# Feed-forward without row products, the overflow branch two experts earlier, and the second block's vectors loaded in the attention

## The chip, the cores and the metric

The kernel runs on one core of a Trainium2 chip. The metric is the device time of one execution in microseconds. A core has a matmul engine (TensorE, PE in the profile, its weight loads PEld), VectorE (DVE), ScalarE (ACT), GpSimd (POOL) and SyncE (SP), which issues the DMA transfers. Each engine runs its own queue in order; semaphores tie the queues together.

## The reference

The model takes x of 256 tokens by 1024, in float32. A first block has two layers: a state-space mixer (layer 0) and a differential attention (layer 1), each followed by a mixture of 32 experts of which every token uses two, with layer norms between. A second block has two layers of a three-part attention and a gated feed-forward. What the change touches:

```python
def hier_moe(x, w_group, w_expert, w_gate, w_up, w_down):     # twice; 32 experts, top 2
    ...
    h = jax.nn.silu(xb @ w_gate[e]) * (xb @ w_up[e])          # 1024 -> 512
    return h @ w_down[e]                                      # 512 -> 1024

def rms_norm(x, g):
    y = xf * lax.rsqrt(jnp.mean(xf * xf, axis=-1, keepdims=True) + NORM_EPS_2)
    return (y * g).astype(x.dtype)

# second block, twice
h = rms_norm(x, g_ffn[l])
u = causal_dwconv(h @ w_up[l], conv_w[l], conv_b[l])          # 1024 -> 5632, three taps over the tokens
gate, up = u[..., :D_FF], u[..., D_FF:]                       # D_FF = 2816
x = x + (jax.nn.silu(gate) * up) @ w_down[l]
```

## The kernel before

The stages follow each other: state-space layer (to about 262 us of the profile), first mixture (to 706), attention (to 850), second mixture (to 1295), then twice an attention mixer and a feed-forward layer, and a last norm. All queues' orders are set when the program is built: a scheduler simulates the engines and orders each queue, so an edit can shift neighbours too.

**Weights** come in pages of 1 MB through `ws`: SyncE issues a load as soon as a page is free and runs ahead of the use by as many pages as there are. `ws.take` and `ws.give` lend a page to other uses.

**Precision.** A float32 weight is split into a high part (ScalarE's cast, line 247) and the rest (a subtraction, line 225, in `low`). Three matmuls, high by high, high by low and low by high (lines 426 to 428), make a product. `low` sends every fourth subtraction to GpSimd and the others to VectorE; with `fast` all go to VectorE. Four buffers hold split weights.

**The mixture** (`moe`). For each expert e: `gate_up` (line 1036) multiplies the gathered tokens with two 1 MB pages each of the gate and up weights, `hidden` forms the gated product, `down` (line 1090) multiplies with the down weights of the expert before. An expert takes up to 32 tokens in this loop. If any expert has more, `overflow` does the rest: all engines load the longest count (line 1162) and take or skip a branch (line 1163) whose body holds the whole code for long experts. Before, it stands behind the last expert, in `moe_layer`, and behind the loads of the next stage's weights; the next thing is `normalize` on the sums `out` (statistics line 519, factors lines 337, 338 and 524, normalized copies line 534 on ScalarE and 536 on VectorE, then transposes, line 204).

**The vectors of the second block** (convolution taps, biases, norm gains) come as rows of 128 numbers: `columns` loads them into staging tiles (line 320) and `finish` transposes these on the matmul engine, copies the result (line 329) and halves some of it (line 2072). `prepare_block2` is a generator that the second mixture resumes at experts 4, 20, 24, 28 and at the end: the loads of layer 0 at the first, those of layer 1 at the second.

**The feed-forward** (`ffn`). xT holds x times the gain, split, by features. The norm's factor `row` is one number per token and is multiplied into the product afterwards. Eleven iterations each take two pages of up weights: 8 weight splits, 96 matmuls into two PSUM accumulators (gate and up), then per accumulator `ff_y` = accumulator times row (line 1742, VectorE), and on two halves of it one tap on ScalarE (line 1748) and two on VectorE (line 1750); then tanh, a gate product on VectorE (line 1755), the product of both on GpSimd (line 1756) and its split into gT (`put_pair`, lines 1810 and 225).

## Time and profile before

| | us |
|---|---|
| median of 3 timed runs | 1997.39 (1997.09 to 1997.48) |
| profiled execution | 1993.87, its span 1992.1 |
| PE busy in the span | 1763.0 (88%) |
| DVE, ACT, POOL busy | 912.1, 856.4, 387.9 |
| first mixture, 262 to 706 | DMA share 0.99, PE busy 363.0 of 444 |
| second mixture, 850 to 1295 | DMA share 0.99, PE busy 358.6 of 445 |
| attention, 706 to 850 | DMA share 0.70, PE busy 129.7 of 144 |
| up projections, 1442 to 1579 and 1777 to 1915.4 | PE busy 130.2 of 137 and 131.3 of 138.4 |

The span is cut into stages because each has another limit: the mean busy share of an engine over the whole span says little about any of them. "Share" of DMA is that of the 16 DMA engines; a share about 1 with a matmul engine that idles is a stage that waits for weights. In rows with a bracket, the first number is the engine's idle time before the instruction, and behind the arrow stands what ended it. A letter q behind an engine's name is its sequencer.

### The profile page before, as it was taken

How to read it: one execution, taken by the hardware profiler on the slowest of the kernel's cores; microseconds unless marked ns; L12 is line 12 of the kernel's file. 1: busy time of each engine (PE TensorE's matmuls, PEld its weight loads, DVE VectorE, ACT ScalarE, POOL GpSimd, SP SyncE). 2: the span in 40 equal slices, each digit the busy share in tenths (PEclk: the TensorE clock that was granted, in tenths of full speed). 3: DMA queues.
4: the chain of work that ended last, by engine and by line, in shares of the span. 5: the costliest groups of instructions: out<-in, count | busy, mean ns of one | idle time of the engine just before them, and what ended most of it. 6: DMA issues, size and time to landing. Idle time of an engine off the chain costs nothing. (4 is left out here: it accounts for less than half of the span.)

```text
span 1992.1 us, 36677 instructions
## 1 busy us (share of the span) xinstructions
PE 1763.0 (88%) x14641; PEld 1388.7 (70%) x14642; DVE 912.1 (46%) x2077; ACT 856.4 (43%) x1940; POOL 387.9 (19%) x329
## 2 busy tenths in 40 slices
PE   8999999787877779999787777779999999999998
PEld 7989876444544467776454444367899997789998
DVE  7888621000100068711000000069589947868983
ACT  5656533121222245633212122256656645656653
POOL 1444300000000023100000000033244423334441
PEclk9999999888989889999889898989999999999999
DMA  9634779999999994799999999974245544424540
GB/s 300 205 127 173 300 307 418 419 418 419 419 419 419 417 335 170 287 368 419 419 419 419 419 373 419 414 264 140 86 156 172 219 145 152 148 86 158 177 174 22
DMA packets 163053, 563.77 MB, mean 283 GB/s; under 512 B 17597, under 2 KB 78652, under 8 KB 114236
## 3 DMA queue, kind: packets, MB, share of 16 engines
q1 hardware_dynamic: 162732, 561.29, 72.8%
q8 instruction: 118, 1.93, 0.4%
q14 instruction: 59, 0.48, 0.1%
q10 hardware_dynamic: 144, 0.07, 0.0%
HBM read 560.27 MB, written 1.05 MB: 282 GB/s over the span
## 5 line engine op out<-in xcount | busy, mean ns | idle before, releaser
L247 ACT CAST w<-w 128x512 fp32r<-128x512 f32 (+1 forms) x592 | 351.6, 610 | 234.2 <-PE acc L256 77.0
L1036 PE MATMUL tr<-w,xe 128*32 128x256 f32 x4096 | 333.5, 426 | 120.3 <-DMA w<-in_moe_w_up_dram 85.5
L225 DVE TENSOR_TENSOR w<-w,w 128x512 fp32r<-128x512 f32 (+1 forms) x450 | 334.1, 755 | 136.8 <-ACT w L247 136.4
L1036 PEld LDWEIGHTS tr<-w,xe 128*32 128x32 f32 x4096 | 150.1, 119 | 273.5 <-DMA w<-in_moe_w_up_dram 120.1
L225 POOL TENSOR_TENSOR w<-w,w 128x512 fp32r<-128x512 f32 (+1 forms) x142 | 199.1, 1402 | 433.0 <-ACT w L247 417.6
L428 PE MATMUL acc<-w,w 128*128 128x256 f32 x960 | 258.1, 286 | 14.8 <-DVE w L225 9.7
L426 PE MATMUL acc<-w,w 128*128 128x256 f32 x960 | 266.6, 283 | 1.5 <-ACT w L247 1.5
L427 PE MATMUL acc<-w,w 128*128 128x256 f32 x960 | 266.4, 283 | 0.0
L428 PEld LDWEIGHTS acc<-w,w 128*128 128x128 f32 x960 | 175.6, 190 | 20.7 <-DVE w L225 14.6
L1071 DVE SCALAR_TENSOR_TENSOR hT<-hT,tr 128x128 f32<-128x128 f32 x64 | 18.4, 288 | 364.1 <-ACT hT L1070 364.1
L426 PEld LDWEIGHTS acc<-w,w 128*128 128x128 f32 x960 | 182.3, 190 | 2.4 <-ACT w L247 1.9
L427 PEld LDWEIGHTS acc<-w,w 128*128 128x128 f32 x960 | 182.4, 190 | 0.5
L1090 PE MATMUL tr<-w,hT 128*32 128x256 f32 x2048 | 154.1, 408 | 30.3 <-DMA w<-in_moe_w_down_dram 22.4
L1045 ACT COPY gu<-tr 128x256 f32<-128x256 f32 x64 | 23.8, 372 | 350.5 <-PE tr L1036 350.5
L255 PE MATMUL acc<-w,w 128*128 128x512 f32 (+3 forms) x416 | 161.4, 390 | 11.1 <-DVE w L225 10.9
L1096 ACT ACTIVATE w<-tr,sw 32x256 f32<-32x256 f32 x248 | 115.6, 466 | 115.4 <-PE tr L1090 98.9
L256 PE MATMUL acc<-w,w 128*128 128x512 f32 (+3 forms) x416 | 153.9, 379 | 0.0
L980 POOL CAST oh<-oh 128x192 fp32r<-128x192 f32 x16 | 5.6, 349 | 738.6 <-DVE oh L977 722.3
L254 PE MATMUL acc<-w,w 128*128 128x512 f32 (+3 forms) x416 | 146.5, 388 | 3.0 <-ACT w L1820 2.0
L478 PE MATMUL acc<-w,w 128*128 128x256 f32 x480 | 134.1, 283 | 0.0
L477 PE MATMUL acc<-w,w 128*128 128x256 f32 x480 | 133.7, 284 | 0.0
L479 PE MATMUL acc<-w,w 128*128 128x256 f32 x480 | 131.7, 285 | 1.5 <-POOL w L225 1.2
(401 smaller groups left out, 2888.6 us busy)
## 6 DMA issues: line engine op xcount, KB each, us to landing
w<-in_moe_w_gate_dram SPq DMA_DIRECT2D x128, 1024.0 KB, 17.6
w<-in_moe_w_up_dram SPq DMA_DIRECT2D x126, 1024.0 KB, 19.9
w<-in_moe_w_down_dram SPq DMA_DIRECT2D x126, 1024.0 KB, 19.9
w<-in_w_up_dram SPq DMA_DIRECT2D x88, 512.0 KB, 5.0
w<-in_w_down_dram SPq DMA_DIRECT2D x22, 1024.0 KB, 6.5
w<-in_w_in_dram SPq DMA_DIRECT2D x18, 1024.0 KB, 8.7
w<-in_ssm_w_in_dram SPq DMA_DIRECT2D x16, 1024.0 KB, 7.6
w<-in_attn_w_qkv_dram SPq DMA_DIRECT2D x12, 1024.0 KB, 10.8
```

Of the source, the lines that this page charges most:

```text
L225: eng.tensor_tensor(lo, x, hi.bitcast(F32), op=ALU.subtract)
L247: self.nc.scalar.copy(hi, w)
L254: mm(out, lhs[0], rhs[0], start=start, stop=False)
L255: mm(out, lhs[0], rhs[1], start=False, stop=False)
L256: return mm(out, lhs[1], rhs[0], start=False, stop=stop)
L426: mm(o, hi[:, ws], xh, start=st, stop=False, skip_group_check=True)
L427: mm(o, hi[:, ws], xl, start=False, stop=False, skip_group_check=True)
L428: mm(o, lo[:, ws], xh, start=False, stop=en, skip_group_check=True)
L477: mm(o, w[0][:, cols], xh, start=start and c % 2 == 0, stop=False, skip_group_check=True)
L478: mm(o, w[0][:, cols], xl, start=False, stop=False, skip_group_check=True)
L1036: mm(p[32 * c:32 * c + 32, :S], xe[:, k, j * SLOTS:(j + 1) * SLOTS], ws[c // 2][0][:, o:o + S], start=k == 0, stop=k == 7)
L1090: mm(pd[quarter(c), :S], hT[:, f % 2, f // 2, :], wt[:, jj * D + c * S:jj * D + (c + 1) * S], start=f == 0, stop=f == 3)
```

## The change

Three parts, in one diff:

1. In `ffn` all subtractions of weight splits and of gT go to VectorE. After the matmuls of iteration 1 xT is built anew with the row factor in it (8 products on VectorE, four casts and four subtractions), so from iteration 2 on there is no `ff_y`: taps read the accumulators in PSUM. The pages of gT are lent when first written.
2. `overflow` is called ahead of the gate and up product of expert 30 and not after the mixture.
3. The loads for both layers' vectors are issued in the attention, ahead of the loads for the second mixture, with four staging tiles; their transposes stand behind the attention's heads. The copies behind the transposes move from VectorE to ScalarE (for all vectors), the halving from VectorE to GpSimd. `prepare_block2` yields three times in their place.

```diff
@@ -326,7 +326,7 @@
                 self.transpose(pt[:, :m], st[:m, :])
-                nc.vector.tensor_copy(fm[:, t * P:t * P + m], pt[:, :m])
+                nc.scalar.copy(fm[:, t * P:t * P + m], pt[:, :m])

@@ -407,14 +407,14 @@
-    def feat_product(self, x, n):
+    def feat_product(self, x, n, fast=False):
...
-                hi, lo = self.split_w(w[:, j * n:(j + 1) * n])
+                hi, lo = self.split_w(w[:, j * n:(j + 1) * n], fast)
@@ -1124,6 +1124,8 @@
                     next(meanwhile, None)
+            if e == NE - 2:
+                self.overflow(L, out, n, gb, wov, cnt, most)
             gu = gate_up(cur[0], j, lambda: gather(cur[1], cur[0], 4) if e == 0 else None, e == 1)
@@ -1729,18 +1731,31 @@
         own = self.lent()
         row = self.over_tokens(self.rms(x, own.page(), self.tr()))
...
         cw, cb = col["conv_w"], col["conv_b"]
-        gT = FeatureMajor(self, NFC)
+        gT = FeatureMajor(self, NFC, later=True)
+        early = 2
         for i in range(NFC // 2):
-            acc = self.feat_product(xT, 512)
+            acc = self.feat_product(xT, 512, True)
+            if i == early - 1:
+                xT.back()
+                xT = FeatureMajor(self, 8)
+                for k in range(0, 8, 2):
+                    t = self.tmp([P, 512], "ff_x")
+                    for j in range(2):
+                        V.scalar_tensor_tensor(t[:, j * S:(j + 1) * S], x[:, (k + j) * S:(k + j + 1) * S],
+                                               col["g_ffn"][:, k + j:k + j + 1], row, op0=ALU.mult, op1=ALU.mult)
+                    xT.put_pair(k, t, fast=True)
             uv = [self.tmp([P, 2, S], f"ff_{n}") for n in "gu"]
             for a, t, c0 in zip(acc, uv, (0, NFC)):
-                y = self.tmp([P, 2, S], "ff_y")
-                V.tensor_tensor(y, a.rearrange("p (j t) -> p j t", j=2), row.unsqueeze(1).to_broadcast([P, 2, S]),
-                                op=ALU.mult)
+                y = a.rearrange("p (j t) -> p j t", j=2)
+                if i < early:
+                    y = self.tmp([P, 2, S], "ff_y")
+                    V.tensor_tensor(y, a.rearrange("p (j t) -> p j t", j=2), row.unsqueeze(1).to_broadcast([P, 2, S]),
+                                    op=ALU.mult)
                 for j in range(2):
@@ -1754,7 +1769,7 @@
             nc.gpsimd.tensor_tensor(g, g, u, op=ALU.mult)
-            gT.put_pair(2 * i, g)
+            gT.put_pair(2 * i, g, fast=True)
         xT.back()
@@ -1781,10 +1796,18 @@

-    def __init__(self, net, nk):
+    def __init__(self, net, nk, later=False):
         self.net, self.parts = net, {}
         self.lent = [net.lent() for _ in range(0, nk, 8)]
-        self.tiles = [[l.page((None, F32, F32R)[self.PARTS]) for _ in range(self.PARTS)] for l in self.lent]
+        self.tiles = []
+        if not later:
+            self.pages(len(self.lent))
+    def pages(self, n):
+        for l in self.lent[len(self.tiles):n]:
+            self.tiles.append([l.page((None, F32, F32R)[self.PARTS]) for _ in range(self.PARTS)])

@@ -1801,9 +1824,10 @@

-    def put_pair(self, k, pt, scale=None, bias=None):
+    def put_pair(self, k, pt, scale=None, bias=None, fast=False):

         nc, net = self.net.nc, self.net
+        self.pages(k // 8 + 1)
         o = (k % 8) * S
@@ -1811,7 +1835,7 @@
             else:
-                net.low(lo, pt, hi)
+                net.low(lo, pt, hi, fast)
             return
@@ -1937,11 +1961,10 @@
         ws.grow(one, 1)
-        out, rest = net.moe(L, h, acc, net.mix_gb[L], net.slot_gb[L], hd, meanwhile)
+        out = net.moe(L, h, acc, net.mix_gb[L], net.slot_gb[L], hd, meanwhile)
         assert ws.shrink(more) == extra and all(ws.shrink(p) == 1 for p in (one, *late))
...
         ws.fill(7)
-        net.overflow(L, out, *rest)
         if upto == 3 + 3 * L:
@@ -1994,6 +2017,10 @@

+    got["gb"] = [col[f"ln_ffn_{i}1"] for i in "gb"]
+    block2 = [block2_columns(net, l, cp) for l in range(2)]
+    got["col"] = [c for c, _ in block2]
     def affine():
@@ -2001,17 +2028,13 @@
     net.diff_attention(xT, *got["rot"], got["lam"], col["subln"].to_broadcast([P, 8]), oT, affine)
+    for _, finish in block2:
+        finish()
     end(pa)
...
     def prepare_block2():
-        got["gb"] = [col[f"ln_ffn_{i}1"] for i in "gb"]
-        got["col"] = []
-        for l in range(2):
-            c, finish = block2_columns(net, l, cp)
-            got["col"].append(c)
+        for _ in range(3):
             yield
-            finish()
-        yield
         ws.keep(1)
@@ -2063,13 +2086,13 @@
         ("g_ffn", one("g_ffn_2")), ("g_q", one("g_q_lat_2")), ("g_kv", one("g_kv_lat_2"))]
-        + [("g_final", rows(A["g_final_2"].unsqueeze(0)))] * l, cp)
+        + [("g_final", rows(A["g_final_2"].unsqueeze(0)))] * l, cp, 4)

...
         for t in [col["conv_w"][:, j * 2 * NFC:j * 2 * NFC + NFC] for j in range(3)] + [col["conv_b"][:, :NFC]]:
-            net.nc.vector.tensor_scalar(t, t, 0.5, None, op0=ALU.mult)
+            net.nc.gpsimd.tensor_scalar(t, t, 0.5, None, op0=ALU.mult)

```

SyncE in the second mixture, before: the staging loads of layer 1 (line 320) stand between the experts' loads (line 373).

```order
L373 DMA w_9228<-in_moe_w_up_dram 128x2048
L320 DMA colstage<-in_conv_w_dram 128x128
L373 DMA w_9238<-in_moe_w_gate_dram 128x2048
L320 DMA colstage<-in_conv_w_dram 4x128
L320 DMA colstage<-in_conv_b_dram 44x128
L320 DMA colstage<-in_g_attn_dram 8x128
L320 DMA colstage<-in_g_ffn_dram 8x128
L320 DMA colstage<-in_g_q_lat_dram 2x128
L320 DMA colstage<-in_g_kv_lat_dram 1x128
L320 DMA colstage<-in_g_final_dram 8x128
L373 DMA w_9302<-in_moe_w_up_dram 128x2048
```

SyncE in the attention, after: the same loads stand behind the two loads of a norm's vectors, with the last loads of the attention's weights (line 385) behind them.

```order
L320 DMA colstage<-in_conv_w_dram 4x128
L320 DMA colstage<-in_conv_b_dram 44x128
L320 DMA colstage<-in_g_attn_dram 8x128
L320 DMA colstage<-in_g_ffn_dram 8x128
L320 DMA colstage<-in_g_q_lat_dram 2x128
L320 DMA colstage<-in_g_kv_lat_dram 1x128
L320 DMA colstage<-in_g_final_dram 8x128
L385 DMA w_6323<-in_attn_w_qkv_dram 128x4x512
L385 DMA w_6357<-in_attn_w_qkv_dram 128x4x512
L385 DMA w_6520<-in_attn_w_qkv_dram 128x4x512
```

What moved: fifteen small loads, seven of layer 0 (which stood ahead of the second mixture's first loads) and eight of layer 1, now stand in one row.

TensorE at the end of the first mixture, before (`hT` and `last` are expert 31's; `w_64` the normalized tokens): the branch stands between the last sum and the next stage's transposes.

```order
L204 MATMUL tr<-cst,gu 128x128 x2
L1090 MATMUL tr<-w_5532,hT 32x256 x8
L1090 MATMUL tr<-w_5545,hT 32x256 x8
L1106 MATMUL acc<-last 128x256 x16
L1162 TENSOR_LOAD most
L1163 COMPARE_AND_BRANCH
L204 MATMUL tr<-cst,w_64 128x128 x16
```

TensorE around expert 28's last matmuls, after: `L1164` and `L1165` are the load and the branch.

```order
L1036 MATMUL tr<-w_5323,xe 32x256 x2
L1090 MATMUL tr<-w_5325,hT 32x256 x8
L204 MATMUL tr<-cst,gu 128x128 x2
L991 MATMUL tr<-eye_r,oh 128x128 x2
L1090 MATMUL tr<-w_5343,hT 32x256 x8
L1164 TENSOR_LOAD most
L1165 COMPARE_AND_BRANCH
```

And TensorE at the mixture's end, after.

```order
L204 MATMUL tr<-cst,gu 128x128 x2
L1090 MATMUL tr<-w_5532,hT 32x256 x8
L1090 MATMUL tr<-w_5545,hT 32x256 x8
L1106 MATMUL acc<-last 128x256 x16
L204 MATMUL tr<-cst,w_64 128x128 x16
L254 MATMUL acc<-w_6060,w_6113 128x512
```

What moved: the branch, from behind line 1106 to ahead of the next gate and up product; the transposes follow on the last sum.

VectorE in a middle iteration of the first feed-forward, before (`ff_g` and `ff_u` are the two halves, `col` the taps).

```order
L225 TENSOR_TENSOR w_10588<-w_12811,w_10588 128x512
L1742 TENSOR_TENSOR ff_y<-acc,rs_row 128x512 x2
L1750 SCALAR_TENSOR_TENSOR ff_g<-ff_y,col_7814,ff_g 128x255 x2
L1750 SCALAR_TENSOR_TENSOR ff_g<-ff_y,col_7814,ff_g 128x254
L225 TENSOR_TENSOR w_10587<-w_12896,w_10587 128x512
L1750 SCALAR_TENSOR_TENSOR ff_g<-ff_y,col_7814,ff_g 128x254
L1750 SCALAR_TENSOR_TENSOR ff_u<-ff_y,col_7814,ff_u 128x255 x2
L225 TENSOR_TENSOR w_10587<-w_12896,w_10587 128x512
L1750 SCALAR_TENSOR_TENSOR ff_u<-ff_y,col_7814,ff_u 128x254
L1755 SCALAR_TENSOR_TENSOR ff_g<-ff_s,ff_g 128x512
L1750 SCALAR_TENSOR_TENSOR ff_u<-ff_y,col_7814,ff_u 128x254
```

And after; line 1765 is the tap, line 1770 the gate product.

```order
L225 TENSOR_TENSOR w_12843<-ff_g,w_12842 128x512
L225 TENSOR_TENSOR w_10588<-w_12963,w_10588 128x512
L1765 SCALAR_TENSOR_TENSOR ff_g<-acc,col_6170,ff_g 128x255
L1765 SCALAR_TENSOR_TENSOR ff_g<-acc,col_6170,ff_g 128x254
L225 TENSOR_TENSOR w_10588<-w_12963,w_10588 128x512
L1765 SCALAR_TENSOR_TENSOR ff_u<-acc,col_6170,ff_u 128x255
L1765 SCALAR_TENSOR_TENSOR ff_g<-acc,col_6170,ff_g 128x255
L1765 SCALAR_TENSOR_TENSOR ff_u<-acc,col_6170,ff_u 128x254
L225 TENSOR_TENSOR w_10587<-w_13044,w_10587 128x512
L1765 SCALAR_TENSOR_TENSOR ff_g<-acc,col_6170,ff_g 128x254
L225 TENSOR_TENSOR w_10587<-w_13044,w_10587 128x512
```

What moved: the two `ff_y` are gone, taps take `acc` for their source, and more subtractions stand between them. GpSimd has in that stage only the gated products (line 1771 after).

## Rows read from the trace of the kernel before

**Rows 1.** stretches: busy time (instructions) per engine, clock, DMA share, GB/s.

```profile
1150.00:1155.00 5.00, 5.00 (x50) 4.30 (x53) 0.82 (x2) 1.39 (x4) 0.00 (x0) 1.00 0.59 233
1155.00:1160.00 5.00, 1.75 (x24) 0.67 (x14) 0.58 (x2) 1.56 (x4) 0.00 (x0) 0.90 0.46 142
1165.00:1290.00 125.00, 94.69 (x964) 56.59 (x958) 8.50 (x31) 27.75 (x67) 3.59 (x10) 0.94 1.01 419
```

**Rows 2.** the SyncE queue in that stretch: start, length, DMA issue.

```profile
1141.73 0.30 SPq L320 DMA_DIRECT2D colstage<-in_conv_w_dram  x1
...
1154.18 0.22 SPq L320 DMA_DIRECT2D colstage<-in_g_kv_lat_dram  x1
...
1156.87 0.36 SPq L373 DMA_DIRECT2D w<-in_moe_w_up_dram  x1
```

**Rows 3.** line 1163, the branch: nanoseconds min/median/max, first and last start.

```profile
L1163 DVEq COMPARE_BRANCH  x2: 68/70/72, 705.6 to 1294.8; - x2
L1163 PEldq COMPARE_BRANCH  x2: 6280/6314/6348, 706.1 to 1295.3; - x2
```

**Rows 4.** timeline after the first mixture's last expert; in brackets idle, releaser.

```profile
709.68 0.16 DVE L524 SCALAR_TENSOR_TENSOR ln_nm<-ln_mv,rs_r 128x1 f32<-128x1 f32 x1 [0.38 <-POOL rs_r L338]
...
711.32 1.21 DVE L524 SCALAR_TENSOR_TENSOR ln_nm<-ln_mv,rs_r 128x1 f32<-128x1 f32 x1 [0.66 <-POOL rs_r L338]
712.63 2.39 ACT L534 ACTIVATE w<-acc,ln_nm,rs_r 128x256 f32<-128x256 f32 x5 [3.86 <-PEq L1163]
...
713.25 1.15 PE L204 MATMUL tr<-cst,w 128*128 128x128 f32 x4 [7.21 <-ACT w L534]
```

**Rows 5.** a stretch of one expert's weights near the first mixture's end.

```profile
671.00:686.00 15.00, 9.23 (x102) 4.18 (x102) 0.57 (x2) 3.34 (x9) 0.78 (x2) 0.89 1.01 419
```

**Rows 6.** a stretch in the middle of the attention heads.

```profile
785.00:845.00 60.00, 57.89 (x337) 47.48 (x335) 44.56 (x144) 37.95 (x105) 11.67 (x13) 1.00 0.69 266
```

**Rows 7.** the staging tiles' transposes, all seven of the program.

```profile
L204 PE MATMUL tr<-cst,colstage x7: 221/273/284, 22.0 to 1172.6; 128*128 128x128 f32 x3, 48*128 48x48 f32 x1, 65*128 65x65 f32 x1, 67*128 67x67 f32 x1
```

**Rows 8.** both up projections without iteration 0, and iterations 2, 3 alone.

```profile
1456.95:1578.63 121.68, 116.76 (x966) 114.50 (x965) 111.18 (x176) 75.04 (x139) 53.47 (x32) 1.00 0.50 166
1468.71:1480.12 11.41, 11.41 (x98) 11.39 (x97) 11.41 (x19) 7.68 (x14) 5.64 (x4) 1.00 0.47 153
1480.12:1493.30 13.18, 12.08 (x99) 11.54 (x97) 10.80 (x19) 7.06 (x13) 5.76 (x4) 1.00 0.52 167
1792.80:1915.38 122.58, 118.26 (x968) 116.25 (x967) 110.77 (x175) 76.54 (x142) 58.21 (x34) 1.00 0.50 166
```

**Rows 9.** VectorE in the first up projection: count, busy us, mean ns, idle before.

```profile
L225 DVE TENSOR_TENSOR w<-w,w 128x512 fp32r<-128x512 f32 x59 | 46.1, 802 | 3.1 <-ACT w L247 3.0
L1750 DVE SCALAR_TENSOR_TENSOR ff_u<-ff_y,col,ff_u 128x254 f32<-128x254 f32 x20 | 13.5, 679 | 0.0
...
L1742 DVE TENSOR_TENSOR ff_y<-acc,rs_row 128x512 f32<-128x512 f32 x20 | 12.8, 677 | 0.0
...
L1750 DVE SCALAR_TENSOR_TENSOR ff_g<-ff_y,col,ff_g 128x254 f32<-128x254 f32 x20 | 10.3, 524 | 0.0
L1755 DVE SCALAR_TENSOR_TENSOR ff_g<-ff_s,ff_g 128x512 f32<-128x512 f32 x10 | 6.8, 677 | 0.0
```

**Rows 10.** GpSimd there.

```profile
L225 POOL TENSOR_TENSOR w<-w,w 128x512 fp32r<-128x512 f32 x20 | 31.8, 1591 | 47.2 <-ACT w L247 46.5 <-DMA w<-in_w_up_dram 0.7
L1756 POOL TENSOR_TENSOR ff_g<-ff_g,ff_u 128x512 f32<-128x512 f32 x10 | 20.4, 2038 | 20.2 <-DVE ff_g L1755 19.8 <-DVE ff_u L1750 0.4
```

**Rows 11.** a run of VectorE taps that read PSUM, in the state-space layer.

```profile
134.88 2.03 DVE L678 SCALAR_TENSOR_TENSOR cv_a<-acc,col,cv_a 128x255 f32<-128x255 f32 x5
```

**Rows 12.** pairs of splits on VectorE, and GpSimd beside the first.

```profile
1503.86 2.38 DVE L225 TENSOR_TENSOR w<-w,w 128x512 fp32r<-128x512 f32 x2
...
1504.02 1.67 POOL L1756 TENSOR_TENSOR ff_g<-ff_g,ff_u 128x512 f32<-128x512 f32 x1 [0.96 <-DVE ff_g L1755]
...
1576.91 1.28 DVE L225 TENSOR_TENSOR w<-w,w 128x512 fp32r<-128x512 f32 x2
```

More of the change, by code (lines that the diff above doesn't have):

```diff
@@ L303, in late_constants, with columns @@
         self.constants(t, first, end)
-    def columns(self, name, arrays, pool=None):
+    def columns(self, name, arrays, pool=None, bufs=2):
         nc = self.nc
@@ L317, in columns @@
                 if r == 0:
-                    stages.append(self.tmp([P, P], "colstage"))
+                    stages.append(self.tmp([P, P], "colstage", bufs=bufs))
                 m = min(n - done, P - r)
@@ L1155, in moe @@
         self.ws.give(self.ws.kept.popleft())
-        return out, (n, gb, wov, cnt, most)
+        return out
     def overflow(self, L, out, n, gb, wov, cnt, most):
```

## The prediction

> **What bounds the kernel now.** I read the table of stretches first, because a change in four places is priced by four stages. In the two expert mixtures the DMA engines are full: from 1165 to 1290 us their share is 1.01 at 419 GB/s while the matmul engine works 94.7 of 125 us [rows 1]. There, only DMA time counts. In the attention (785 to 845) the matmul engine works 57.9 of 60 us [rows 6]; there, an added matmul costs its length. In the two up projections of the feed-forward layers neither DMA (share 0.50) nor the clock (1.00) binds. Iterations 1 to 10 take 121.68 and 122.58 us [rows 8]; all have 96 matmuls, yet one takes 11.41 us, in which the matmul engine never idles, and the next 13.18. At 11.41 each they would take 114.1, so 121.68 + 122.58 - 228.2 = 16.1 us are stalls. What stalls them is VectorE: 111.2 busy of 121.7 us, and GpSimd's long pieces of the same chain.
>
> **Small loads in the second mixture.** The SyncE queue shows the second layer's staging loads of l=1 (line 320) from 1136.76, some 2.5 us apart: each waits for an older transfer to land, so from 1141.73 to 1154.18 almost no 1 MB weight load is issued; the next goes out at 1156.87 [rows 2]. Consequence: the DMA share falls to 0.59 and 0.46 in two stretches of 5 us, afterwards it is full to the mixture's end [rows 1]. Lost: (1.01 - 0.59 + 1.01 - 0.46) x 5 = 4.85 us. The new place has these loads in the attention, where the DMA engines are at 0.69 [rows 6] and SyncE runs ahead of the matmul engine. I take **-4.9**; ends 0 (the hole comes back elsewhere) and -5.5 (the missing bytes at 419 GB/s: 186 + 277 GB/s for 5 us each are 2.3 MB).
>
> **The branch.** The overflow test costs the matmul engine 6.28 and 6.35 us although it only skips the body; VectorE needs 70 ns for it [rows 3]. After the last expert, ScalarE's normalized copies wait for that engine's branch: the factors for the first half of the tokens are ready at 709.84, the copies start at 712.63 [rows 4]. Without the branch the first half can start 2.8 us earlier. The second half can't: its factor is ready at 711.32 + 1.21 = 712.53. Half of the copies ahead gives between 0 and 2.8, I take 1.5, twice: **-3.0**.
> At the new place the branch stands between expert 28's last matmul and expert 30's first. There the engine has 9.23 us of work in 15 us of weights [rows 5], 5.8 us free per expert, and about two experts' weights still to come (some 30 us, 11 us free). A stop of 6.3 us therefore delays the weights' consumer, not the weights, as long as pages for them are free; it is caught up before the last weights land. I take **0**; if nothing is caught up it is +6.3 twice (a rival below). SyncE's own stop at the branch moves as well: it waits there for the older transfers to land, which now stands ahead of six of the attention's weight loads, not behind them; two transfers of 1 MB still run meanwhile, so I charge nothing.
> The page "Runtime: NRT & Kernel Launch" of the Trainium skill (Instruction fetch mechanics) says that a taken branch whose target lies outside the fetched window stops its engine until the target's page has come. The 6.3 us against 70 ns agree with that, and by it the price recurs in full at the new place, hidden or not; it does not shrink with the new neighbours.
>
> **The vectors' finish.** Seven transposes of the staging tiles exist, median 273 ns [rows 7]; four of them move into the attention, behind the heads, where the matmul engine is the bound: 4 x 0.273 = **+1.1**. Bounds: 0 (they fill a gap: 2.1 of 60 us there are idle) and +2.5 (each followed by a wait for ScalarE's copy of its bank). The eight scalings go to GpSimd, which has 11.7 busy of 60 us; the copies to ScalarE (38 of 60): nothing.
>
> **The feed-forward.** Per iteration VectorE has now 59/10 of the weights' splits and three of four of the gate's own, 6.6 splits, 8 taps, 2 products ff_y, one gate product. Unhindered prices: a pair of splits 1.28, so 0.64 [rows 12]; five taps from PSUM 2.03, so 0.41 [rows 11]; ff_y and the gate product 0.64 like a split (same size; their means are 0.677 [rows 9]). That makes 4.2 + 3.3 + 1.3 + 0.6 = 9.4 us, but it is busy for 11.1: the 1.7 us beside it come from collisions with GpSimd, 53.5/10 = 5.35 us per iteration [rows 8], as in the pair of splits that took 2.38 beside GpSimd's product and 1.28 without [rows 12]. So 0.32 us lost per us of GpSimd.
> After: 9 splits, 8 taps, no ff_y, one gate: 5.8 + 3.3 + 0.6 = 9.7. GpSimd keeps one product, 2.04 [rows 10], so 0.65 is lost: 10.3 us, under the matmul engine's 11.41. Also gone are the splits that GpSimd did in 1.59 against VectorE's 0.80 [rows 9, 10], for which the matmul engine waited. I leave 0.05 per iteration, 1 us in all: -15.1.
> On the other side stands the rebuilding of xT with the row factor, once per layer at i=1: 8 products of 128x256 (0.41) and 4 splits (0.64) on VectorE, 5.8 us, and 4 casts on ScalarE, which has room (75 of 122 us). Iteration 1 keeps its ff_y, so VectorE needs 10.3 + 1.3 + 5.8 = 17.4 us against 11.4: 6.0 behind. Four split buffers of 1.43 us of matmuls each hold 5.7 us when full, and taps can come late. The trace shows no such burst; the ends are 0 (full buffers) and 6.0 (empty ones). With 1.1 us of room per iteration they are more than half full by my reckoning, 3.5 us: I take 2.5, twice: +5.0. Sum of the feed-forward: **-10.1**, with ends -16.1 and about -3 (no cover, 2 x 6.0).
> On collisions the Trainium skill goes further ("SBUF — State Buffer", Who interferes with whom): a VectorE instruction with two SBUF operands is shut out for the whole of a GpSimd instruction that reads SBUF, one with a single SBUF operand not at all. The slow and the quick pair of splits fit it. By it the new taps, which read PSUM, never collide, and a split loses up to 2.04 us per iteration: 9.7 + 2.0 = 11.7, slightly over 11.41. That would leave some 0.3 us of stall in 18 iterations, 5 us of the 15; it is the half-gain rival below, and one reason for its chance.
> Iteration 0 and the down projection's start keep their waits; with splits only on VectorE, and another order, they can move by 1 us either way.
>
> **Sum.** -4.9 - 3.0 + 1.1 - 10.1 = -16.9. The profiled run took 1993.87 (span 1992.1 and 1.8 around it), so 1977.0. The median of the timed runs, 1997.39, is 3.5 above that profile; with the same distance 1980.5, **1980**.
>
> **Rivals.**
> *Half the gain.* The xT burst has no cover (+12 for two layers), or each iteration keeps a long collision. Feed-forward -3 to -5, total -10 to -12: **1987**. For it: VectorE holds 9 of 9 splits and has only 1.1 us of room per iteration.
> *VectorE becomes the bound: slower.* Its mean prices stay what they are: 9 x 0.80 + 8 x 0.60 (taps between 0.524 and 0.679) + 0.68 = 12.7 us for each of 9 iterations per layer, and the burst is unhidden, 11.4 + 6. Per layer 114.3 + 17.4 = 131.7 against 122.1: +19 for both, with the other terms -6.8: +12.3, **2010**. Its place is the VectorE queue; it decides from about 12 us per iteration (with the 17.4, 125.5 per layer is where the gains elsewhere are used up). Against it: those means hold the collisions with 5.35 us of GpSimd, of which 3.3 go.
> *The branch isn't absorbed.* The matmul engine's 6.3 us, with pages freed late, hold up the last weight loads in both mixtures: -16.9 + 12.6 = -4.3, **1993**. Against it: the 5.8 us free per expert.
> *The loads' hole reappears.* 15 small loads in one row hold up the attention's last weights as they held the experts': without the -4.9 it is **1985**. Against it: the transfers there are busy for 0.69 of the time, so a late one catches up [rows 6].
> *More.* The burst is free and the feed-forward runs at 11.4 us: -22, **1975**.
>
> **How the numbers follow.** Forecast 0.55 (own range 1977 to 1985); half the gain 0.15; more 0.08; hole 0.07; branch 0.08; slower 0.07. From no change 0.2% (4 us) can be told. Faster: 0.55 + 0.15 + 0.08 + 0.07, and 0.01 of the branch, 0.86; same: 0.07 of the branch and none else; slower 0.07. The range 1970 to 1993 leaves out the slower case and half of the branch's; its low end is -16.1, -5.5, -5.6 (two branches at 2.8) and 0, so -27.
>
> **What will show it.** The stretch that had share 0.59 and 0.46 is at 1.01. After the last expert ScalarE's copies start within 0.5 us of their factor, with no release by the matmul engine's branch; that branch, still 6 us, stands some 35 us earlier, and the weights' DMA share stays 1.01 beside it. Iterations 3 to 10 take 11.4 to 11.6 us, VectorE 10.0 to 10.6 busy, taps at 0.41 to 0.48; around iteration 2 stands one stall of 1 to 4 us. Wrong would be: VectorE at 11.4 of 11.4 in every iteration, a DMA share under 1 in the mixtures' last 40 us, or small loads 2.5 us apart with a matmul engine waiting for the attention's weights.

## The result and the profile after

The changed kernel takes 1968.26 us (median of 4, 1966.69 to 1968.89) against 1997.24; the ratio is 0.9859, interval 0.9842 to 0.9876. Forecast were 1980 and a range of 1970 to 1993: the direction was right, the gain of 29 us is 1.7 times the forecast 17, and the time lies below the range. The profiled execution fell from 1993.87 to 1968.73, by 25.1.

The same marks in both traces (the last sum of a mixture, the first product of a stage, the first and last product of the feed-forward layers) split the 25.2 us of span:

| stretch | forecast | measured |
|---|---|---|
| second mixture, first gate product to last sum | -4.9 | -2.0 |
| both mixtures' ends to the next stage's first product, and the first mixer's start | -3.0 | -3.0, -2.5, -1.5 |
| attention | +1.1 | +1.2 |
| feed-forward layers, with the down projections | -10.1 | -8.8, -9.9 |
| state-space layer and first mixture, second mixer, last norm | 0 | +0.5, +1.0, -0.2 |

**Second mixture.** The stretches that answer to [rows 1], after: the hole in the DMA share is gone.

```profile
1150.00:1155.00 5.00, 5.00 (x58) 4.10 (x57) 0.82 (x2) 2.16 (x5) 0.00 (x0) 1.00 1.02 419
1155.00:1160.00 5.00, 2.58 (x25) 0.93 (x24) 0.58 (x2) 0.78 (x3) 0.00 (x0) 0.82 1.01 419
```

**The mixtures' ends.** The timeline that answers to [rows 4]: the factor (line 524), ScalarE's copies (534), the transposes (204).

```profile
709.67 0.16 DVE L524 SCALAR_TENSOR_TENSOR ln_nm<-ln_mv,rs_r 128x1 f32<-128x1 f32 x1 [0.38 <-POOL rs_r L338]
...
709.87 1.93 ACT L534 ACTIVATE w<-acc,ln_nm,rs_r 128x256 f32<-128x256 f32 x4 [0.60 <-DVE ln_nm L524]
...
710.49 1.15 PE L204 MATMUL tr<-cst,w 128*128 128x128 f32 x4 [3.98 <-ACT w L534]
...
712.46 1.44 DVE L536 TENSOR_SCALAR w<-acc,ln_mv,rs_r 128x256 f32<-128x256 f32 x3
712.57 0.56 ACT L534 ACTIVATE w<-acc,ln_nm,rs_r 128x256 f32<-128x256 f32 x1 [0.77 <-DVE ln_nm L524]
```

ScalarE's copies start 0.04 us after the first half's factor; before, 2.8 us after it. The second half has only one copy left for ScalarE and three for VectorE (line 536), so nearly the whole 2.8 us arrives at the transposes.

The branch itself (now line 1165), against [rows 3], and the matmul engine's first instruction behind it in the first and in the second mixture:

```profile
L1165 PEldq COMPARE_BRANCH  x2: 445/3324/6203, 669.8 to 1255.1; - x2
```

```profile
674.23 1.07 PE L1036 MATMUL tr<-w,xe 128*32 128x256 f32 x4 [4.04 <-DVEq L1165]
```

```profile
1261.81 1.07 PE L1036 MATMUL tr<-w,xe 128*32 128x256 f32 x4 [6.12 <-PEq L1165]
```

In the second mixture the engine stands 6.1 us, as before; in the first the branch takes 0.45 us and the engine waits 4.0 for a signal of VectorE's queue. Neither reaches the mixture's end (e10 below).

**Feed-forward.** Stretches of the first and second layer after, which answer to [rows 8]: iteration 0, iterations 1 to 10, one late iteration alone, and iterations 1 to 10 of the second layer.

```profile
1434.69:1448.17 13.48, 12.66 (x106) 12.46 (x105) 12.39 (x22) 8.32 (x17) 5.12 (x4) 1.00 0.35 98
1448.17:1564.82 116.65, 116.31 (x966) 115.80 (x965) 106.78 (x196) 80.79 (x146) 16.22 (x10) 1.00 0.52 170
1541.78:1553.30 11.52, 11.52 (x98) 11.52 (x97) 10.21 (x18) 7.92 (x15) 1.61 (x1) 1.00 0.51 180
1775.65:1890.56 114.91, 114.55 (x967) 114.01 (x966) 107.14 (x196) 80.87 (x146) 16.20 (x10) 1.00 0.53 172
```

Iteration 0 of both layers before, which was not shown:

```profile
1442.04:1456.95 14.91, 13.07 (x107) 12.45 (x106) 12.60 (x18) 8.43 (x17) 8.58 (x7) 1.00 0.43 137
1777.32:1792.80 15.48, 12.65 (x107) 12.45 (x106) 13.03 (x21) 8.39 (x17) 6.79 (x5) 1.00 0.42 136
```

Iterations 1 to 10 fell from 121.7 to 116.65 and from 122.6 to 114.9 us, iteration 0 from 14.91 and 15.48 to 13.48 and 13.47. VectorE is busy 10.2 of 11.52 us. Its lines and GpSimd's in iterations 2 to 10 of the first layer, against [rows 9, 10]:

```profile
L225 DVE TENSOR_TENSOR w<-w,w 128x512 fp32r<-128x512 f32 x75 | 55.2, 742 | 7.7 <-ACT w L247 7.0
...
L1765 DVE SCALAR_TENSOR_TENSOR ff_u<-acc,col,ff_u 128x254 f32<-128x254 f32 x16 | 7.6, 474 | 0.0
...
L1770 DVE SCALAR_TENSOR_TENSOR ff_g<-ff_s,ff_g 128x512 f32<-128x512 f32 x10 | 6.8, 684 | 0.0
```

```profile
L1771 POOL TENSOR_TENSOR ff_g<-ff_g,ff_u 128x512 f32<-128x512 f32 x10 | 16.2, 1622 | 98.8 <-DVE ff_g L1770 83.8 <-DVE ff_u L1765 15.0
```

And what the matmul engine waited for in the first layer and its down projection (us in total, times, longest), before and then after:

```profile
PE acc L428 <- DVE w L225: 4.1, 7, 1.0
PE acc L428 <- POOL w L225: 2.4, 2, 1.2
PE acc L479 <- POOL w L225: 1.2, 1, 1.2
```

```profile
PE acc L428 <- DVE w L225: 1.1, 2, 0.8
```

Before, 3.6 us are splits that GpSimd delivered late (1.2 of them in the down projection, line 479) and 4.1 are VectorE's; after, 1.1 us is left, although VectorE makes all the splits.

### The profile page after: what moved, and what is told of

Same layout as the page of the kernel before. It is cut to its first block, busy times and chain, and to the rows that moved or that the text cites. A ratio compares the mean times of both kernels' runs of the same rounds, so it can differ in the third digit from the quotient of the medians.

```text
span 1966.9 us, 36628 instructions
## 1 busy us (share of the span) xinstructions
PE 1761.8 (90%) x14641; PEld 1391.9 (71%) x14642; DVE 894.3 (45%) x2099; ACT 867.3 (44%) x1955; POOL 304.5 (15%) x288
## 4 chain that ended last, share of the span: by engine, by line
PE 36%; DMA 21%; DVE 4%; ACT 2%; issue 1%; POOL 0%; SPq 0%; DVEq 0%; POOLq 0%; ACTq 0%
DMA w<-in_moe_w_up_dram 12%; DMA w<-in_moe_w_down_dram 9%; PE acc L428 4%; PE acc L255 4%; PE acc L426 4%; PE acc L427 4%; PE acc L256 3%; PE acc L254 3%; PE acc L479 3%; PE acc L477 3%; PE acc L478 3%; PE tr L204 2%; DVE w L225 1%; PE tr L1316 1%; PE tr L1494 1%
## 5 line engine op out<-in xcount | busy, mean ns | idle before, releaser
L247 ACT CAST w<-w 128x512 fp32r<-128x512 f32 (+1 forms) x592 | 357.5, 612 | 274.0 <-PE acc L427 97.4
L225 DVE TENSOR_TENSOR w<-w,w 128x512 fp32r<-128x512 f32 (+2 forms) x494 | 361.1, 740 | 154.6 <-ACT w L247 152.7
L426 PE MATMUL acc<-w,w 128*128 128x256 f32 x960 | 267.1, 284 | 1.6 <-ACT w L247 1.6
L427 PE MATMUL acc<-w,w 128*128 128x256 f32 x960 | 266.8, 283 | 0.0
L428 PE MATMUL acc<-w,w 128*128 128x256 f32 x960 | 258.7, 285 | 3.4 <-DVE w L225 3.2
L225 POOL TENSOR_TENSOR w<-w,w 128x512 fp32r<-128x512 f32 (+2 forms) x98 | 129.3, 1320 | 334.6 <-ACT w L247 311.9
L478 PE MATMUL acc<-w,w 128*128 128x256 f32 x480 | 131.0, 284 | 0.0
L477 PE MATMUL acc<-w,w 128*128 128x256 f32 x480 | 130.4, 284 | 0.0
L1002 PE MATMUL tr<-oh,w 128*128 128x128 f32 x512 | 127.0, 402 | 2.6 <-DVE oh L977 2.6
L1090 PEld LDWEIGHTS tr<-w,hT 128*32 128x32 f32 x2048 | 67.6, 117 | 86.8 <-issue 19.9
```

Of the source, the lines that this page charges most:

```text
L225: eng.tensor_tensor(lo, x, hi.bitcast(F32), op=ALU.subtract)
L247: self.nc.scalar.copy(hi, w)
L426: mm(o, hi[:, ws], xh, start=st, stop=False, skip_group_check=True)
L427: mm(o, hi[:, ws], xl, start=False, stop=False, skip_group_check=True)
L428: mm(o, lo[:, ws], xh, start=False, stop=en, skip_group_check=True)
L477: mm(o, w[0][:, cols], xh, start=start and c % 2 == 0, stop=False, skip_group_check=True)
```

## The experiments

Fifteen runs, four or three kernels together on one chip beside the kernel before (medians there 1997.45, 1996.44, 1995.76 and 1996.36).

| run | median us | ratio to before, interval |
|---|---|---|
| e1 feed-forward alone | 1979.20 | 0.9909 (0.9893 to 0.9925) |
| e2 branch alone | 1990.17 | 0.9966 (0.9955 to 0.9977) |
| e3 vectors alone | 1994.69 | 0.9986 (0.9976 to 0.9996) |
| e4 fast splits alone | 1974.77 | 0.9887 (0.9870 to 0.9904) |
| e5 changed, no rebuild | 1967.67 | 0.9862 (0.9847 to 0.9876) |
| e6 changed, branch at expert 31 | 1976.59 | 0.9902 (0.9888 to 0.9916) |
| e7 rebuild alone | 1991.78 | 0.9978 (0.9967 to 0.9988) |
| e8 changed, iteration 0 as before | 1971.78 | 0.9882 (0.9867 to 0.9897) |
| e9 changed, small loads added | 1969.17 | 0.9871 (0.9855 to 0.9887) |
| e10 changed, no branch | 1969.04 | 0.9868 (0.9851 to 0.9885) |
| e11 changed, rebuild at 4 | 1965.59 | 0.9853 (0.9839 to 0.9867) |
| e12 e5, no GpSimd splits in block 2 | 1964.92 | 0.9841 (0.9827 to 0.9855) |
| e13 changed, small loads held | 1977.80 | 0.9903 (0.9887 to 0.9918) |
| e14 changed again | 1967.89 | 0.9855 (0.9840 to 0.9870) |
| e15 e11, no GpSimd splits in block 2 | 1963.30 | 0.9832 (0.9818 to 0.9845) |

**The three parts alone (e1 to e3).** Each is the kernel before with one of the three parts of the diff.

> Only the feed-forward part. Theory 1 (each part gains at its own place, and the feed-forward gains more than forecast because its first iteration and the start of the down projection are freed too): in the profile the two feed-forward layers are 18 to 19 us shorter, 6 of these in iteration 0 and at the down projections' start; the total is 18 to 19 us below the profile of before. Theory 2 (the feed-forward gained the forecast 10 us and the rest came from new orders around it that all three parts together made): about 10 us.

> Only the branch ahead of expert 30. Theory 1 (ScalarE's normalized copies were the only users of the matmul engine's stop, so nearly the whole 2.8 us is gained at each mixture's end): 5 to 7 us faster, first matmul of the next stage 2.5 to 3 us nearer to the mixture's last one. Theory 2 (half of the copies only, as forecast): 3 us. If the stop is not absorbed at its new place: 0 or slower.

> Only the vectors' loads and their finish. Theory 1 (the hole in the second mixture's weight stream was worth 4.1 us, the four transposes in the attention cost 1 to 1.6 us): 2.5 to 3.5 us faster. Theory 2 (the hole is worth only the 2 us by which the second mixture became shorter): 1 us faster or nothing.

Measured: 18.2, 7.3 and 2.8 us, each with an interval of 2 to 3 us to either side: theory 1 three times, in e2 a little above its range. They add up to 28.3, the whole change brought 29: within that, the parts don't help each other, and no order that only the three together make is needed. In e1's trace the two feed-forward layers are 17.0 us shorter, 6.0 of these in iteration 0 and the down projections. In e2's trace the first product stands 2.9 us nearer to the first mixture's last sum, as in the changed kernel.

**Fast splits without the rebuild (e4, e5), and the rebuild without fast splits (e7).**

```diff
 # e4 (on the kernel before with the feed-forward part), e5 (on the changed kernel)
-        early = 2
+        early = 99
 # e7 (on the kernel before with the feed-forward part)
-            acc = self.feat_product(xT, 512, True)
+            acc = self.feat_product(xT, 512)
-                    xT.put_pair(k, t, fast=True)
+                    xT.put_pair(k, t)
-            gT.put_pair(2 * i, g, fast=True)
+            gT.put_pair(2 * i, g)
```

> The feed-forward's splits all on VectorE, but ff_y stays in all eleven iterations and xT is not rebuilt. By the unhindered prices VectorE needs 9 x 0.64 + 8 x 0.41 + 2 x 0.64 + 0.64 + 0.65 = 11.6 us per iteration against the matmul engine's 11.4 to 11.5. Theory 1 (GpSimd's splits were the stalls, by collisions and by their own 1.6 us): iterations of 11.6 to 11.8 and 10 to 14 us of gain. Theory 2 (the row products were the load that made VectorE late): under 5 us of gain.

> The changed kernel with ff_y kept in all eleven iterations and no rebuilt xT; fast splits, branch and vectors as changed. Theory 1 (the matmul engine is the bound as soon as GpSimd splits nothing; the rebuild only adds a burst of VectorE work): iterations of 11.3 to 11.5 us from iteration 1 on, two feed-forward layers 3 to 4 us shorter than in the changed kernel, 1963 to 1965. Theory 2 (the advantage seen without the rebuild belongs to that kernel's order of instructions): 1968.

> The kernel before with xT rebuilt and taps that read PSUM from iteration 2 on, but every fourth split still on GpSimd. Theory 1 (GpSimd's splits are the stalls, not VectorE's load): the rebuild costs 2 us per layer and gains little, 1993 to 1999, with waits for GpSimd's splits left in the list. Theory 2 (VectorE's load is the stall): ff_y's 1.3 us per iteration are gained, 1980 to 1988.

e4 gained 22.7 us, more than theory 1's 10 to 14 and more than the whole feed-forward part. Its iterations 1 to 9 in the first layer, and VectorE's lines there:

```profile
1455.84:1558.27 102.43, 102.43 (x868) 102.33 (x867) 98.91 (x179) 70.04 (x126) 18.68 (x9) 1.00 0.48 150
```

```profile
L225 DVE TENSOR_TENSOR w<-w,w 128x512 fp32r<-128x512 f32 x72 | 53.7, 766 | 3.6 <-ACT w L247 3.4
L1755 DVE TENSOR_TENSOR ff_y<-acc,rs_row 128x512 f32<-128x512 f32 x18 | 11.5, 678 | 0.0
...
L1763 DVE SCALAR_TENSOR_TENSOR ff_u<-ff_y,col,ff_u 128x254 f32<-128x254 f32 x18 | 8.5, 472 | 0.0
```

The matmul engine never idles in 102.43 us, although ff_y stays and the taps read it from SBUF. A tap takes 0.47 us here, as from PSUM in the changed kernel. The 0.68 of [rows 9] was GpSimd's doing: of the 80 taps before, the 65 that ran without GpSimd at work beside them took 0.47, the 15 beside it 1.23 in the mean. Two rows of before show it; the first of the two taps took 1.52 us:

```profile
1463.50 1.29 POOL L225 TENSOR_TENSOR w<-w,w 128x512 fp32r<-128x512 f32 x1 [5.90 <-ACT w L247]
1463.54 1.92 DVE L1750 SCALAR_TENSOR_TENSOR ff_u<-ff_y,col,ff_u 128x255 f32<-128x255 f32 x2
```

So fast splits suffice; the rebuilt xT adds nothing to them. e5 says the same within the measurement: 1967.67 against 1968.26 and 1967.89, theory 2's number; theory 1's 3 to 4 us did not come. Counted by 96 matmuls, its iterations 1 to 3 are 1.0 and 0.7 us shorter than the changed kernel's, but in the second layer each later one takes 11.52 us against 11.31, and both layers together come out only 0.3 us shorter.

e7 gained 4.7 us, between both theories, and its trace tells why. From iteration 3 on, with GpSimd still splitting, the matmul engine never idles in either layer:

```profile
1483.62:1575.95 92.33, 92.33 (x772) 92.33 (x771) 81.45 (x134) 63.99 (x117) 39.89 (x27) 1.00 0.46 146
1818.73:1911.07 92.34, 92.34 (x772) 92.34 (x771) 80.62 (x130) 63.93 (x115) 39.15 (x27) 1.00 0.45 145
```

Its taps read PSUM there, and GpSimd at work beside them costs them nothing: the 51 in both layers that ran beside it took 0.48 us, the others 0.47. A split of GpSimd's and the two taps in its time:

```profile
1487.40 1.74 POOL L225 TENSOR_TENSOR w<-w,w 128x512 fp32r<-128x512 f32 x1
1487.91 0.47 DVE L1763 SCALAR_TENSOR_TENSOR ff_g<-acc,col,ff_g 128x254 f32<-128x254 f32 x1
1488.30 0.47 DVE L1763 SCALAR_TENSOR_TENSOR ff_u<-acc,col,ff_u 128x255 f32<-128x255 f32 x1
```

What e7 loses stands at the start of a layer: iteration 0 takes 14.9 and 16.9 us, and iterations 1 and 2, with the burst, 26.9 and 28.9 against e5's 23.5. So in the late iterations either edit alone ends the stalls; at the start only the fast splits do. Both runs also have the later pages of gT, which no run has alone; the waits before name splits only, and no load.

**Iteration 0 (e8).**

```diff
-            acc = self.feat_product(xT, 512, True)
+            acc = self.feat_product(xT, 512, i > 0)
```

> The changed kernel with every fourth split of iteration 0 alone back on GpSimd. Theory 1 (iteration 0 was shortened by 1.4 and 2.0 us because GpSimd splits nothing there): iteration 0 back at 14.9 and 15.5 us, 3 to 4 us slower, 1971 to 1972. Theory 2 (it was shortened by the new order): 13.5 us as in the changed kernel, 1968.

```profile
1433.95:1448.93 14.98, 13.19 (x107) 12.57 (x105) 13.32 (x19) 8.44 (x17) 7.95 (x6) 1.00 0.29 88
```

Theory 1: 14.98 and 14.97 us, and 3.5 to 3.9 us slower than the changed kernel: GpSimd's splits, not the new order, had made iteration 0 long.

**The burst (e11).**

```diff
-        early = 2
+        early = 5
```

> The changed kernel with xT rebuilt at iteration 4 instead of 1, so that ff_y stays in five iterations. Theory 1 (the burst costs 1.5 to 2 us per layer wherever it stands, since the split buffers are never more than partly full, and ff_y costs nothing): iterations 4 to 6 at 12 us instead of 1 to 3, same total, 1968. Theory 2 (the burst is dear only because it follows the start of the layer): 1964 to 1966.

Iterations 4 and 5 of the first layer, 96 matmuls each, and the rebuild's products and splits there (duration in ns, first and last start):

```profile
1480.95:1492.47 11.52, 11.52 (x99) 11.52 (x97) 11.52 (x23) 8.30 (x15) 2.25 (x1) 1.00 0.01 1
1492.47:1503.99 11.52, 11.52 (x99) 11.52 (x97) 11.52 (x22) 8.21 (x15) 1.30 (x1) 1.00 0.90 278
```

```profile
L1749 DVE SCALAR_TENSOR_TENSOR ff_x<-w,col,rs_row x8: 467/473/480, 1449.9 to 1485.5; 128x256 f32<-128x256 f32 x8
L225 DVE TENSOR_TENSOR w<-ff_x,w x4: 673/673/674, 1480.2 to 1490.5; 128x512 fp32r<-128x512 f32 x4
```

VectorE is full, but the matmul engine never idles: these iterations take 11.52 us like those beside them, and the rebuild costs the matmul engine nothing in either layer, where iterations 1 and 2 of the changed kernel lost 1.0 us to it in this layer. In the trace theory 2 holds. But it is no longer one burst: the scheduler began it in iteration 1 and spread it over 41 us, against 15 us in the changed kernel (1452 to 1467). So fuller split buffers and the spreading both stand for the cover, and the run doesn't tell them apart. The times can't tell the gain: the ratio is 0.9853 against e14's 0.9855.

**The branch's place (e6, e10).**

```diff
 # e6
-            if e == NE - 2:
+            if e == NE - 1:
 # e10
-            if e == NE - 2:
-                self.overflow(L, out, n, gb, wov, cnt, most)
```

> The changed kernel with the branch ahead of the last expert (31). Theory 1 (the matmul engine catches up its 6.3 us in the time that it would wait for weights, about 5.8 us per expert): with one expert left, 1 to 4 us per mixture show, 1970 to 1976. Theory 2 (the stop is hidden wherever weights are still to come): 1968.

> The changed kernel without the overflow branch (experts with over 32 tokens would not be finished; none has so many here). Theory 1 (ahead of expert 30 the branch is absorbed): no change, 1967 to 1969. Theory 2 (it still costs part of its 6.3 us there, as it costs 5 us ahead of expert 31): 2 to 8 us faster.

Without the branch nothing is gained (1969.04), and the two mixtures take 443.3 and 442.1 us from the first gate product to the last sum, against 442.6 and 443.0 in the changed kernel: at expert 30 the branch is absorbed but for at most 0.9 us. At expert 31 it is not:

```profile
L1165 PEldq COMPARE_BRANCH  x2: 6034/6061/6088, 694.0 to 1283.1; - x2
```

8.3 us slower; the mixtures take 4.2 and 4.9 us longer, more than the expected 1 to 4. Theory 1 has the sign, but not the size: with one expert left, a fifth to a third of the 6 us is caught up.

**The small loads (e9, e13).** Both are the changed kernel with rows of eight small loads, resumed by the second mixture: two rows in e9, three in e13, where each row but the first waits until the tile of the row before was transposed and written back.

```diff
 # e13; e9 has the loads without the transpose and the copy
     def prepare_block2():
+        st = net.tmp([P, P], "colstage", bufs=1)
         for i in range(3):
+            if i:
+                pt = net.tr()
+                net.transpose(pt[:, :107], st[:107, :])
+                nc.scalar.copy(st[:, :107], pt[:, :107])
+            # eight loads of 32, 4, 44, 8, 8, 2, 1 and 8 rows into st
             yield
```

> The changed kernel with two added rows of eight small loads (of 1 to 44 rows of 512 bytes, their data is not used) in SyncE's queue in the second mixture, where the kernel before had its staging loads. Theory 1 (a row of small loads takes the places of large ones among the transfers under way, and costs the mixture the net 2.6 us that removing one brought): about 5 us slower, 1973. Theory 2 (a row costs the whole 4.9 us of missing share): 10 us, 1978. Theory 3 (the small loads were hidden, and the mixture was shorter for another reason): 1968.

> The changed kernel with two rows of eight small loads held in the second mixture: each row waits for a transpose of the tile that the row before filled, so it can't run ahead into the attention as in the run before. Theory 1 (a row costs net 2.6 us): about 5 us slower than the changed kernel, 1973 to 1974. Theory 2 (a row costs the missing share, 4.9 us): 1977 to 1979. Theory 3 (a row costs nothing): 1968.

e9 missed its aim: SyncE ran both rows ahead into the attention, where 16 more small loads cost nothing that can be told (1969.17 against 1968.26; line, shortest, median and longest issue in ns, first and last start):

```profile
L2039 SPq DMA_DIRECT2D colstage<-in_conv_w_dram x16: 223/294/603, 828.2 to 850.5; - x16
```

In e13 the first row again ran ahead into the attention (831 to 845); the two others stood in the mixture, at 1139 and 1203, and the hole came back. The DMA shares beside the first of these and its place in SyncE's queue:

```profile
1150.00:1155.00 5.00, 5.00 (x47) 4.28 (x49) 0.42 (x2) 0.94 (x3) 0.00 (x0) 1.00 0.44 175
1155.00:1160.00 5.00, 1.87 (x28) 0.65 (x20) 0.97 (x3) 2.00 (x5) 0.00 (x0) 1.00 0.44 142
```

```profile
1138.98 17.66 SPq L2044 DMA_DIRECT2D colstage<-in_conv_w_dram  x8
1156.73 0.36 SPq L373 DMA_DIRECT2D w<-in_moe_w_up_dram  x1
```

It is 9.9 us slower than e14 beside it, 4.95 per held row: by the times theory 2, the forecast's price. By the traces only 7.5 us of it lie in the second mixture, from the first gate product to the last sum: 3.8 per row, between theories 1 and 2. The rest lies in stages in which none of the held rows stands, and is not shown to be theirs.

**Which kernel is best (e12, e14, e15).**

```diff
 # e12 on e5, e15 on e11: in low(), switched on ahead of the second block
+        fast = fast or getattr(self, "all_fast", False)
```

> As the changed kernel without the rebuild (1967.7), and every split of the second block's mixers and down projections on VectorE too. The matmul engine waits there for VectorE 2.5 us of 135 and never for GpSimd, so theory 1 (only a split that is late counts): within 2 us of 1967.7. Theory 2 (GpSimd's splits slow VectorE down everywhere by collisions): 4 to 6 us faster, 1962 to 1964.

> The changed kernel itself, beside the two others of this chip: 1968 by both theories; it tells how far single medians of one kernel lie apart from chip to chip, on which the differences of 1 to 4 us between the last kernels rest.

> The changed kernel with xT rebuilt at iteration 4 and every split of the second block on VectorE. Theory 1 (no split that is late is left, each edit frees what it frees alone): 1962 to 1964. Theory 2 (the edits' gains are one and the same): 1965 to 1966.

e14 repeats the changed kernel within 0.4 us. e15 is the fastest: its five runs (1961.85 to 1964.56) all lie under e14's four (1967.20 to 1968.73), 4.6 us by the medians, theory 1's number. In the traces e12's second mixer takes 131.4 us against e5's 134.1, from the last product of one feed-forward layer to the first of the next, although the list of waits named GpSimd nowhere there. That fits collisions that made VectorE late, but wasn't isolated. e12 is 2.8 us under e5, between the two theories, and their intervals overlap.

## Why the prediction was wrong

**The terms, in the trace: 8.3 of the 12.2 us missed** (from the sum's 1980.5). The step that failed is "Iteration 0 and the down projection's start keep their waits": they lost 3.4 us (iteration 0, both layers) and 2.6 us (down projections, from the last up to the last down product 65.3 and 63.7 to 63.1 and 63.3). I had read the 16.1 us of stalls from iterations 1 to 10 only and left out the two ends. In iteration 0 it was GpSimd's splits: e8 puts 3.0 of the 3.4 us on them. In the down projections it was not they alone: e7, in which GpSimd still splits, has 63.4 and 63.1 us there too. All runs with a part of the feed-forward edit share the later pages of gT; whether these or VectorE's lighter load shortened the down projections stays open.
The second is the branch's "half of the copies ahead": 1.5 each, measured 3.0 and 2.5. The second half's factor did come when I said, but with the first half done ScalarE and VectorE share what is left. Another 1.5 us came off the first mixer's start; e2 has them too, but e9, e10 and e13 don't, so they are not shown to be the branch's.
The third is the burst: 2.5 per layer. Iterations 1 to 3 took 1.45 and 1.8 us longer than three late ones, but 0.4 of that is in iteration 1 without a burst as well (11.95 us in e5 and e11); 1.0 and 1.4 are left. That the buffers' filling decides is not shown: e11, in which the rebuild costs nothing, also spread it over a longer time.
The fourth errs the other way, the hole: 4.9 forecast, 2.0 in this pair of traces. Over all traces the second mixture takes 444.1 to 446.0 us in the five kernels with the hole and 441.8 to 443.0 in the ten without (e6 and e13 left out), 3.0 us between the means. Behind the hole the weight loads stand 4.1 us earlier than before, but 1.4 of these are a pause of the kernel before at 1167 (3.9 us from one load to the next instead of 2.5); the changed kernel has a like pause at 1228 (4.3 us), and behind both 2.6 are left. Why the missing 4.9 us of DMA share move the loads by no more stays open.

**The distance of profile and median: 4 us.** I carried the 3.5 us between the profile of before and its median over to the changed kernel, whose profile lies 0.5 above its median. Single runs of the kernel before spread from 1992.4 to 2001.6 in these series; the profile of before was one of the short ones.

**What held.** The mechanism of the feed-forward: 10.3 us of VectorE work per iteration (measured 10.1 to 10.2), taps at 0.475, iterations of 11.3 to 11.5, stalls of 15.1 us gone (12.7 with the burst's 2.4 makes 15.1; that the sizes meet so closely is partly luck). But the argument took both edits for it, and either alone ends the stalls of the late iterations: GpSimd's splits gone in e4, ff_y gone and taps from PSUM in e7. The transposes cost 1.2 for 1.1 in this pair, 0.7 by the means of all traces. The branch is absorbed at expert 30 (e10).

**The rivals.** "VectorE becomes the bound" fell by its premise that the mean durations stay; "half the gain" likewise. The exclusive lock of the Trainium skill's page "SBUF — State Buffer" (Who interferes with whom), one ground for the half gain, let a split lose up to 2.04 us per iteration. The traces agree with it on who collides (taps from SBUF took 1.23 us beside GpSimd, taps from PSUM 0.48), but the loss was smaller: in e4 the 24 splits that ran beside GpSimd's products in the first layer took 0.94 us in the mean against 0.68, which is 0.7 us per iteration, and those in the second 0.70. For 2.2 us of GpSimd per iteration the first is 0.31 us per us, my 0.32. e4's taps, with two SBUF operands, are no test of it: none of the 144 in iterations 1 to 9 ran beside GpSimd. "The branch isn't absorbed" is what e6 shows one expert later. The sentence that the branch's price recurs in full, after the Trainium skill's "Runtime: NRT & Kernel Launch" (Instruction fetch mechanics), agrees with the second mixture (6.2 us) and not with the first (0.45).

## What to carry to other kernels

An engine that helps with every fourth piece of work can cost more than it does: price its pieces by their own length and by what they add to the neighbour's, and try leaving them out before anything is rebuilt around them. Where either of two edits ends a stall alone, their gains don't add: try each by itself. Count the stalls of a loop with its first round and its exit, not only in the steady state. A stop that can't be removed belongs where the engine would wait anyway, with enough of that waiting still to come: two experts before the end hide 6 us, one does not.

## What the hardware showed beside it

- The same branch on the matmul engine takes 0.35 to 0.49 us in one place (ahead of expert 30 in the first mixture) and 5.9 to 6.5 in the others. In e14, the changed kernel itself, it took 2.8 in the place where that had 0.45, so the program alone doesn't decide; what does was not tried.
- At a granted clock of 1.00 the 96 matmuls of a full iteration take 11.52 us in one layer and 11.31 in the other, 120.0 and 117.8 ns each, and the same again in e14. Which of the two a layer gets changes with the kernel (both 11.52 in e5), and in e11's second layer the time slides from 11.52 to 11.39; why was not tried. Over a layer this is 2 us, as much as some of the edits.
